# The first 20 microseconds of a streaming encoder: norm of the memory tokens, weight splits and bias tables in another order

## The chip, the cores and the metric

The kernel runs on one core of a Trainium2 chip. A time is that of the device for one launch, in microseconds. The core has five engines with a queue of instructions each, worked off in order: TensorE (PE: matmuls and transposes into PSUM), VectorE (DVE), ScalarE (ACT), GpSimd (POOL) and SyncE (SP), which issues most of the DMA transfers; POOL issues some too. An engine waits at an instruction until its operands are there, and everything behind it in that queue waits with it.

## The reference

One layer of a hybrid encoder on 2048 prompt frames and 8 x 16 sample frames, D_MODEL = 1024, all in float32. The part that matters here comes first in the kernel and is small:

```
def memory_kv(mem, g_mem, w_mk, w_mv):      # mem: 256 tokens x 1024
    m = rmsnorm(mem, g_mem)                 # mem * rsqrt(mean(mem^2) + EPS) * g_mem
    mk = (m @ w_mk).reshape(B, N_MEM, MEM_HEADS, MEM_HEAD_DIM)
    mv = (m @ w_mv).reshape(B, N_MEM, MEM_HEADS, MEM_HEAD_DIM)
    return mk, mv
```

After it come the projections of the frames, chunked band attention with a bias looked up by relative distance (`rel_bias`, 8 heads x 257), a causal depthwise convolution, the output projection, cross-attention into mk and mv, and a SwiGLU feed-forward layer.

## The kernel before

Float32 products are made of three matmuls: each operand is split into a high part (rounded to the type that TensorE takes at full rate) and a low part (the rest), and `mm3` (lines L281 to L283) adds high x high, high x low and low x high in PSUM. So each weight block of 128 x 1024 is loaded into one of three buffers `wf`, ScalarE makes the high part (`wload`, L275), and VectorE or GpSimd the low part (L276).

The phases follow each other: memory tokens (`phase_mem`), projections (`phase_proj`), attention, output projection, cross-attention, feed-forward. The instructions of all phases are given to a planner that simulates a timeline, with its own costs, and writes each engine's order; so the source's order is not the chip's, and work of a later phase may stand between that of an earlier one. `issue_after(x)`, which the changed kernel uses, forces an order: what is written under it comes behind instruction x on x's engine.

`phase_mem` does this:

- SP loads token tile 0 (128 tokens x 1024), the norm weight `g_mem_kv` spread over 128 partitions by a broadcasting transfer of 512 KB (`gain`, L360), token tile 1, and then blocks of `w_mk`.
- For each tile, `prenorm` squares and sums the rows on ScalarE (L306), makes the rsqrt on GpSimd (L298, L299), scales by it and by the norm weight on VectorE (L313), transposes eight 128 x 128 pieces on TensorE into one PSUM tile of 4 KB per partition (L316), and splits all eight at once: high part by ScalarE (L317), low part by VectorE (L318).
- For each of the eight blocks of `w_mk`, 24 matmuls (8 x `mm3`) give 128 rows of the transposed keys for all 256 tokens. The sum goes to SBUF on VectorE (L406), is split again (L407, L408), and is transposed back for the output (L394, L396). The low parts of blocks 0 and 1 are made on GpSimd, those of the others on VectorE.
- The keys are multiplied with `w_mqT`, head by head: 8 pieces of 6 matmuls per head, whose sums VectorE copies out (L426), and each head's 1 MB is stored to DRAM as `f1s` (L427). The output buffer exists twice, so head 2 waits for the store of head 0. Then the same for `w_mv` and `w_mo`.

`bias_tables` makes the table for the relative bias: SP loads the reversed bias (L249), VectorE builds rows of 767 values (L250 to L252), SP stores them to DRAM as `fd` (L254), and GpSimd issues a copy DRAM to DRAM (L259) that spreads them to `toep`, 2.5 MB, which attention reads much later. `phase_proj` halves the convolution's weights and two norm vectors on VectorE (L459, L461). The planner put both among the first instructions of VectorE.

Of the kernel before, what the change touches and what calls it, by code (L numbers as in the profile page):

```python
# [8 lines left out]
F32 = mybir.dt.float32  # L9
# [3 lines left out]
ALU = mybir.AluOpType  # L13
# [4 lines left out]
P = 128  # L18
D = 1024
# [6 lines left out]
NM = 256  # L26
# [14 lines left out]
MID = 4  # L41
TR0 = [12, 8]
MM = [12, 14, 4, 6]
HP = 100
HP2 = 200

# [90 lines left out]
class Build:  # L137
# [107 lines left out]
    def bias_tables(self, pool):  # L245
        nc, A = self.nc, self.A
        fb = self.t(pool, [H, 768], F32, "fb")
        rv = self.t(pool, [H, 256], F32, "rv")
        nc.sync.dma_start(rv[:, :], A["rel_rev"])  # L249
        nc.vector.memset(fb[:, :511], 0.0)  # L250
        nc.vector.tensor_scalar(fb[:, :511], fb[:, :511], rv[:, 0:1], None, ALU.add)
        nc.vector.tensor_copy(fb[:, 511:767], rv[:, :])  # L252
        fd = self.t(self.dpool, [H, 768], F32, "fd")
        nc.sync.dma_start(fd[:, :767], fb[:, :767])  # L254

        yield
        toep = self.t(self.dpool, [H, P, 5 * P], F32, "toep")
        f0 = fd[0, :]
        nc.gpsimd.dma_start(toep[:, :, :], bass.AP(f0.tensor, f0.offset + 127, [[768, H], [-1, P], [1, 5 * P]]))  # L259
        self.toep = [toep[h] for h in range(H)]  # L260
# [4 lines left out]
            return A[name + "_sample"][:, :]  # L265
        return A[name + "_prompt"][t * P:(t + 1) * P, :]

    def wload(self, src, hi=None, lo=None):
        nc = self.nc
        wf = self.t(self.w, [P, D], F32, "wf")  # L270
        self.last_load = nc.sync.dma_start(wf[:, :], src)
        if hi is None:
            hi = self.t(self.w, [P, D], F32R, "wh")
            lo = self.t(self.w, [P, D], F32R, "wl")
        nc.scalar.copy(hi[:, :], wf[:, :])  # L275
        self.lo_engine.tensor_tensor(lo[:, :], wf[:, :], hi[:, :].bitcast(F32), ALU.subtract)  # L276
        return hi, lo

    def mm3(self, ps, lh, ll, rh, rl, start, stop, **kw):
# [40 lines left out]
    def prenorm_halves(self, pool, pspool, xt, gbc, hi, lo):  # L320

        nc = self.nc
        r = self.rms(pool, xt[:, :])
        nc.vector.scalar_tensor_tensor(xt[:, :], xt[:, :], r[:, :], gbc[:, :], ALU.mult, ALU.mult)
        for k0 in range(0, KC, 4):
            ps = self.t(pspool, [P, 4, P], F32, "tr")
            for k in range(4):
                nc.tensor.transpose(ps[:, k, :], xt[:, (k0 + k) * P:(k0 + k + 1) * P], self.ident[:, :])
            sl = slice(k0, k0 + 4)
            nc.scalar.copy(hi[:, sl, :], ps[:, :, :])  # L330
            nc.vector.tensor_tensor(lo[:, sl, :], ps[:, :, :], hi[:, sl, :].bitcast(F32), ALU.subtract)

    def postnorm(self, pool, y, xt, gbc, dst, dma=None, bufs=2):
        nc = self.nc
# [28 lines left out]
    def phase_mem(self):  # L363
        nc, A = self.nc, self.A
        fa, fb = self.fa, self.fb
        pool = (Region().lay(self.sbF, 26, ("xt", 4, 2), ("gbc", 4, 1), ("yf", 1, 3), ("fb", 3, 1), ("rv", 1, 1))
                .lay(self.sbF, 24, ("junk", 2, 1)).lay(fb, 0, ("f1o", 8, 2))
                .lay(fa, 0, ("f2o", 8, 2), ("ot", 4, 2), ("ss", 0.03125, 6), ("rstd", 0.03125, 6))
                .lay(self.sbR, 24, ("mh", 8, 1), ("ml", 8, 1), ("yh", 8, 2), ("yl", 8, 2)))
        ps_mm = ps_tr = self.psa  # L370
        self.lo_engine = nc.vector
        xts = []
        for i in range(2):
            xt = self.t(pool, [P, D], F32, "xt", 2)
            nc.sync.dma_start(xt[:, :], A["mem_prompt"][i * P:(i + 1) * P, :])
            xts.append(xt)
            if i == 0:
                gbc = self.gain(pool, "g_mem_kv", "gbc")
        tables = self.bias_tables(pool)
        mh = self.t(pool, [P, KC, NM], F32R, "mh")  # L380
        ml = self.t(pool, [P, KC, NM], F32R, "ml")
        for i in range(2):
            self.prenorm(pool, ps_tr, xts[i], gbc, mh[:, :, i * P:(i + 1) * P], ml[:, :, i * P:(i + 1) * P])
        for which, wn, on in ((0, "w_mk", "new_mem_k_prompt"), (1, "w_mv", "new_mem_v_prompt")):
            yh = self.t(pool, [P, KC, NM], F32R, "yh", 2)
            yl = self.t(pool, [P, KC, NM], F32R, "yl", 2)
# [9 lines left out]
                    nc.scalar.copy(ot[i][:, j * P:(j + 1) * P], pt[:, i, :])  # L396

            for j in range(KC):
                self.lo_engine = nc.gpsimd if which == 0 and j < 2 else nc.vector
                wh, wl = self.wload(A[wn][j])  # L400
                ps = self.t(ps_mm, [P, 512], F32, "mm")
                for k in range(KC):
                    c = slice(k * P, (k + 1) * P)
                    self.mm3(ps[:, :NM], wh[:, c], wl[:, c], mh[:, k, :], ml[:, k, :], k == 0, k == KC - 1)
                yf = self.t(pool, [P, NM], F32, "yf", 3)
                nc.vector.tensor_copy(yf[:, :], ps[:, :NM])  # L406
                nc.scalar.activation(yh[:, j, :], yf[:, :], AF.Copy, scale=scale)  # L407
                nc.vector.scalar_tensor_tensor(yl[:, j, :], yf[:, :], scale, yh[:, j, :].bitcast(F32),  # L408
                                               ALU.mult, ALU.subtract)
# [36 lines left out]
    def phase_proj(self):  # L446
# [14 lines left out]
        nc.vector.tensor_scalar(half[:, :, :], cvec[:, 1:3, :], 0.5, None, ALU.mult)  # L461
        us = self.t(pool, [P, 4, DEC_B, HALO + DEC_S], F32, "us")

        def conv_halo():
# [1233 lines left out]
```

## Time and profile before

| what | us |
|---|---|
| median of 3 runs | 3012.31 (3011.44 to 3014.95) |
| the profiled execution | 3017.42 |
| its span, first to last instruction | 3015.6 |
| TensorE busy in the span | 2946.0 (98%) |
| VectorE busy | 2137.0 (71%) |
| ScalarE busy | 1358.3 (45%) |
| GpSimd busy | 1418.9 (47%) |

The tables of the profile name a group of instructions by line, engine, operation, output<-input and shape; `sbf`, `sbr`, `sbx` and `flexb` are the arenas in SBUF, `psb` is PSUM. Where a row of groups has two numbers and a bar, they are busy time and mean duration in ns, and behind the bar stands the idle time of the engine before them with what ended it. A timeline row has start and duration in us. A row of stretches has each engine's busy time and count, then the granted clock of TensorE (1.00 is full; before the first record of the clock, 1.00 is shown too), the mean busy share of the 16 DMA engines and the rate in GB/s.

### The profile page before, as it was taken

Reading aid. Unit: us, or ns where it says so; the run is one execution under the profiler, and the core shown is the slowest. Engines: PE = TensorE matmul, PEld = TensorE weight load, DVE = VectorE, ACT = ScalarE, POOL = GpSimd, SP = SyncE. Lnnn points to the kernel's source line nnn. Section 1 sums busy time; section 2 is a strip of 40 time slices with the busy share of each in tenths; the row PEclk is TensorE's granted clock in tenths of the full one; section 3 lists DMA queues with packets and bytes.
Section 4 is the critical chain, followed back from the end, with each engine's and each line's share of the span. In section 5 each row is a group of like instructions: output and inputs, shape, how many; then the busy total and the mean of one; then the engine's idle time right before and its main releaser. Section 6 shows DMA issues by size and latency. Waiting matters only on the chain.

```text
span 3015.6 us, 46098 instructions
## 1 busy us (share of the span) xinstructions
PE 2946.0 (98%) x16924; PEld 2712.9 (90%) x16924; DVE 2137.0 (71%) x3086; ACT 1358.3 (45%) x2729; POOL 1418.9 (47%) x1338
## 2 busy tenths in 40 slices
PE   7999999979999999999999999999999999999998
PEld 7999999969998888788878999999999999888887
DVE  6697795857786466535357887888788999655566
ACT  4535365657785345323334333433334444433433
POOL 1267496721113234226356655555555775524413
PEclk9999999989899999999999999999999999999999
DMA  8635353644534556324246433444434445756674
GB/s 295 246 112 179 96 165 110 202 167 172 181 135 153 175 190 216 128 68 147 74 166 210 138 128 132 166 166 153 154 125 160 144 139 187 260 187 207 220 230 149
DMA packets 197695, 500.10 MB, mean 166 GB/s; under 512 B 19349, under 2 KB 84765, under 8 KB 188627
## 3 DMA queue, kind: packets, MB, share of 16 engines
q1 hardware_dynamic: 182539, 427.53, 42.9%
q0 software_dynamic: 14928, 69.61, 6.2%
q8 instruction: 133, 2.18, 0.3%
q14 instruction: 95, 0.78, 0.1%
HBM read 365.97 MB, written 141.81 MB: 168 GB/s over the span
## 4 chain that ended last, share of the span: by engine, by line
PE 38%; DMA 4%; DVE 3%; issue 3%; POOL 3%; ACT 0%; SPq 0%; DVEq 0%; POOLq 0%; ACTq 0%
PE psb L283 12%; PE psb L282 12%; PE psb L281 12%; DMA sbf<-in_w_down_dram 2%; POOL sbf L1538 1%; PE psb L289 1%; DMA sbf<-x 1%; PE psb L1393 1%; DVE sbr L1416 0%; DMA sbf<-in_w_gate_dram 0%; DVE sbr L1608 0%; POOL sbf L338 0%; DMA hn<-sbf 0%; DVE sbr L1542 0%; DVE flexb L1478 0%
## 5 line engine op out<-in xcount | busy, mean ns | idle before, releaser
L281 PE MATMUL psb<-sbr 128*128 128x384 f32 (+3 forms) x2808 | 942.6, 337 | 4.1 <-DVE flexb L426 1.4
L282 PE MATMUL psb<-sbr 128*128 128x384 f32 (+3 forms) x2356 | 806.2, 342 | 3.4 <-DVE sbr L318 3.3
L283 PE MATMUL psb<-sbr 128*128 128x512 f32 (+3 forms) x1848 | 632.8, 344 | 3.7 <-DVE sbr L1608 3.6
L281 PEld LDWEIGHTS psb<-sbr 128*128 128x128 f32 x2808 | 530.9, 189 | 33.9 <-DVE flexb L426 2.1
L283 PE MATMUL psb<-sbr,sbx 128*128 128x384 f32 (+2 forms) x1484 | 477.2, 322 | 0.0
L282 PEld LDWEIGHTS psb<-sbr 128*128 128x128 f32 x2356 | 445.5, 189 | 30.6 <-DVE sbr L318 3.6
L283 PEld LDWEIGHTS psb<-sbr 128*128 128x128 f32 x1848 | 348.0, 189 | 33.2 <-DVE sbr L1608 6.3
L289 PE MATMUL psb<-sbr 128*128 128x512 f32 x1200 | 295.3, 394 | 2.7 <-POOL sbr L1251 1.4
L1416 DVE TENSOR_TENSOR sbr<-sbf,sbr 128x512 fp32r<-128x512 f32 x258 | 262.5, 1020 | 38.6 <-ACT sbr L1415 37.7
L1415 ACT CAST sbr<-sbf 128x512 fp32r<-128x512 f32 x258 | 159.3, 620 | 278.7 <-PE psb L282 228.8
L283 PEld LDWEIGHTS psb<-sbr,sbx 128*128 128x128 f32 x1484 | 281.2, 190 | 0.1
L523 DVE SCALAR_TENSOR_TENSOR psb<-sbf,psb 128x768 f32<-128x768 f32 (+1 forms) x290 | 264.3, 911 | 6.2
L289 PEld LDWEIGHTS psb<-sbr 128*128 128x128 f32 x1200 | 222.2, 189 | 48.5 <-POOL sbr L1251 1.8
L1608 DVE TENSOR_TENSOR sbr<-sbf,sbr 128x384 fp32r<-128x384 f32 (+2 forms) x242 | 166.4, 711 | 93.6 <-ACT sbr L1607 92.4
L276 POOL TENSOR_TENSOR sbx<-sbf,sbr 128x1024 fp32r<-128x1024 f32 x62 | 158.7, 2563 | 79.9 <-ACT sbr L275 76.4
L1607 ACT CAST sbr<-sbf 128x384 fp32r<-128x384 f32 (+2 forms) x242 | 112.4, 483 | 171.6 <-PE psb L282 149.4
L1538 POOL TENSOR_TENSOR sbf<-sbf 128x512 f32<-128x512 f32 x77 | 107.0, 1392 | 165.5 <-DMA sbf<-in_w_down_dram 163.6
L533 POOL TENSOR_TENSOR flexb<-flexb,flexb 128x128 f32<-128x128 f32 (+1 forms) x180 | 169.4, 942 | 23.1 <-ACT flexb L532 12.3
L281 PE MATMUL psb<-sbr,sbx 128*128 128x384 f32 (+1 forms) x524 | 170.6, 327 | 1.5 <-ACT sbx L1415 0.8
L1415 ACT CAST sbx<-sbf 128x512 fp32r<-128x512 f32 x153 | 94.7, 620 | 162.2 <-PE psb L282 147.4
L1416 DVE TENSOR_TENSOR sbx<-sbf,sbx 128x512 fp32r<-128x512 f32 x153 | 155.3, 1016 | 16.3 <-ACT sbx L1415 16.0
L1410 POOL TENSOR_TENSOR sbf<-sbf 128x512 f32<-128x512 f32 x66 | 96.9, 1468 | 107.3 <-DVE sbr L1416 50.5
(339 smaller groups left out, 6269.2 us busy)
## 6 DMA issues: line engine op xcount, KB each, us to landing
af<-flexb SPq DMA_DIRECT2D x33, 1344.0 KB, 5.7
sbf<-in_w_down_dram SPq DMA_DIRECT2D x154, 256.0 KB, 3.8
sbf<-in_w_gate_dram SPq DMA_DIRECT2D x66, 512.0 KB, 3.5
sbf<-in_w_up_dram SPq DMA_DIRECT2D x66, 512.0 KB, 3.9
sbf<-af SPq DMA_DIRECT2D x85, 384.0 KB, 4.1
sbf<-x SPq DMA_DIRECT2D x49, 512.0 KB, 4.0
sbf<-in_w_in_dram SPq DMA_DIRECT2D x48, 512.0 KB, 4.1
sbr<-ks POOLq DMA_DIRECT2D x16, 1024.0 KB, 8.5
```

Of the source, the lines that this page charges most:

```text
L276: self.lo_engine.tensor_tensor(lo[:, :], wf[:, :], hi[:, :].bitcast(F32), ALU.subtract)
L281: nc.tensor.matmul(ps, lh, rh, start=start, stop=False, **kw)
L282: nc.tensor.matmul(ps, lh, rl, start=False, stop=False, **kw)
L283: nc.tensor.matmul(ps, ll, rh, start=False, stop=stop, **kw)
L289: nc.tensor.matmul(y[o], l, r[:, o * 512:(o + 1) * 512], start=start and x == 0, stop=stop and x == 2)
L523: nc.vector.scalar_tensor_tensor(acc if w < CW - 1 else o, src(w), cwt[:, j, w:w + 1], acc, ALU.mult, ALU.add)
L533: nc.gpsimd.tensor_tensor(o, o, v, ALU.add)
L1415: nc.scalar.copy(hs[j][:, :], src[j])
L1416: nc.vector.tensor_tensor(ls[j][:, :], src[j], hs[j][:, :].bitcast(F32), ALU.subtract)
L1538: nc.gpsimd.tensor_tensor(acc[:, :], acc[:, :], q[:, :], ALU.add if s > 0 else ALU.subtract)
L1607: nc.scalar.copy(ch[:, m], a[:, x, m])
L1608: nc.vector.tensor_tensor(cl[:, m], a[:, x, m], ch[:, m].bitcast(F32), ALU.subtract)
```

## The change

- The norm weight is loaded as one row of 4 KB, first in SP's queue, and the two token tiles come right behind it. Two matmuls of a column of ones (1 x 128) with the row (1 x 512 each) spread it over 128 partitions in PSUM, where VectorE reads it when it scales.
- TensorE makes six transposes of the identity, with no use of the result, before these two matmuls and six after them.
- The tokens are transposed and split by PSUM bank: four pieces, then a high part and a low part of 128 x 512 (`prenorm_halves`, which `phase_proj` already uses), instead of eight and 128 x 1024.
- The low part of `w_mk` block 0 is made in two halves on GpSimd; those of block 1 (from GpSimd) and block 2 go to VectorE. High and low parts of blocks 1 and 2 are put behind the last splits of the tokens on ScalarE and VectorE.
- The load for the bias table comes after the loads for the first `w_mqT` head, and the three VectorE instructions of the table come after the last sum of the `w_mk` product; so the store of `fd` and the copy to `toep` come later too. In the order written for SP the load moves from place 7 to 22 and the store from 17 to 30.
- The halving of the convolution's vectors is put behind the last sum of the `w_mv` product.

Apart from these, the planner's order differs around the place where attention meets the output projection (some 200 matmuls, and instructions of ScalarE, VectorE and SP beside them), with the same instructions in it.

```diff
+WARM = (6, 0, 6)
...
-        nc.sync.dma_start(rv[:, :], A["rel_rev"])
-        nc.vector.memset(fb[:, :511], 0.0)
-        nc.vector.tensor_scalar(fb[:, :511], fb[:, :511], rv[:, 0:1], None, ALU.add)
-        nc.vector.tensor_copy(fb[:, 511:767], rv[:, :])
+        with self.tc.issue_after(self.last_load.ins):
+            nc.sync.dma_start(rv[:, :], A["rel_rev"])
+        with self.tc.issue_after(self.first_sum.ins):
+            nc.vector.memset(fb[:, :511], 0.0)
+            nc.vector.tensor_scalar(fb[:, :511], fb[:, :511], rv[:, 0:1], None, ALU.add)
+            nc.vector.tensor_copy(fb[:, 511:767], rv[:, :])
...
-    def wload(self, src, hi=None, lo=None):
+    def wload(self, src, hi=None, lo=None, parts=1):
...
-        self.lo_engine.tensor_tensor(lo[:, :], wf[:, :], hi[:, :].bitcast(F32), ALU.subtract)
+        for c in (slice(0, 512), slice(512, D)) if parts == 2 else (slice(0, D),):
+            self.lo_engine.tensor_tensor(lo[:, c], wf[:, c], hi[:, c].bitcast(F32), ALU.subtract)
...
     def phase_mem(self):
...
+        gain = self.t(pool, [1, D], F32, "gain")
+        nc.sync.dma_start(gain[:, :], A["g_mem_kv"].unsqueeze(0))
         xts = []
         for i in range(2):
             xt = self.t(pool, [P, D], F32, "xt", 2)
             nc.sync.dma_start(xt[:, :], A["mem_prompt"][i * P:(i + 1) * P, :])
             xts.append(xt)
-            if i == 0:
-                gbc = self.gain(pool, "g_mem_kv", "gbc")
+        ones = self.t(pool, [1, P], F32, "ones")
+        nc.vector.memset(ones[:, :], 1.0)
+        gbc = self.t(Region().lay(self.ps, 0, ("gbc", 4, 1)), [P, D], F32, "gbc")
+        warm = self.t(Region().lay(self.ps, 4, ("warm", 0.5, 1)), [P, P], F32, "warm")
+        event = None
+        for o in range(3):
+            with self.tc.issue_after(event.ins) if event else ExitStack():
+                for _ in range(WARM[o]):
+                    nc.tensor.transpose(warm[:, :], self.ident[:, :], self.ident[:, :])
+            if o < 2:
+                oc = slice(o * 512, (o + 1) * 512)
+                event = nc.tensor.matmul(gbc[:, oc], ones[:, :], gain[:, oc], start=True, stop=True)
...
-            self.prenorm(pool, ps_tr, xts[i], gbc, mh[:, :, i * P:(i + 1) * P], ml[:, :, i * P:(i + 1) * P])
+            splits = self.prenorm_halves(pool, ps_tr, xts[i], gbc, mh[:, :, i * P:(i + 1) * P], ml[:, :, i * P:(i + 1) * P])
...
-                self.lo_engine = nc.gpsimd if which == 0 and j < 2 else nc.vector
-                wh, wl = self.wload(A[wn][j])
+                self.lo_engine = nc.gpsimd if which == 0 and j == 0 else nc.vector
+                with ExitStack() as behind:
+                    for event in splits if which == 0 and j in (1, 2) else ():
+                        behind.enter_context(self.tc.issue_after(event.ins))
+                    wh, wl = self.wload(A[wn][j], parts=2 if which == 0 and j == 0 else 1)
...
-                nc.vector.tensor_copy(yf[:, :], ps[:, :NM])
+                self.first_sum = nc.vector.tensor_copy(yf[:, :], ps[:, :NM])
...
-        nc.vector.tensor_scalar(cwt[:, :, :], cwt[:, :, :], 0.5, None, ALU.mult)
         half = self.t(pool, [P, 2, 4], F32, "half", 1)
-        nc.vector.tensor_scalar(half[:, :, :], cvec[:, 1:3, :], 0.5, None, ALU.mult)
+        with self.tc.issue_after(self.first_sum.ins):
+            nc.vector.tensor_scalar(cwt[:, :, :], cwt[:, :, :], 0.5, None, ALU.mult)
+            nc.vector.tensor_scalar(half[:, :, :], cvec[:, 1:3, :], 0.5, None, ALU.mult)
```

More of the change, by code (lines that the diff above doesn't have):

```diff
@@ L329, in prenorm_halves @@
             sl = slice(k0, k0 + 4)
-            nc.scalar.copy(hi[:, sl, :], ps[:, :, :])
-            nc.vector.tensor_tensor(lo[:, sl, :], ps[:, :, :], hi[:, sl, :].bitcast(F32), ALU.subtract)
+            last = (nc.scalar.copy(hi[:, sl, :], ps[:, :, :]),
+                    nc.vector.tensor_tensor(lo[:, sl, :], ps[:, :, :], hi[:, sl, :].bitcast(F32), ALU.subtract))
+        return last
     def postnorm(self, pool, y, xt, gbc, dst, dma=None, bufs=2):
@@ L365, in phase_mem @@
         fa, fb = self.fa, self.fb
-        pool = (Region().lay(self.sbF, 26, ("xt", 4, 2), ("gbc", 4, 1), ("yf", 1, 3), ("fb", 3, 1), ("rv", 1, 1))
-                .lay(self.sbF, 24, ("junk", 2, 1)).lay(fb, 0, ("f1o", 8, 2))
+        pool = (Region().lay(self.sbF, 26, ("xt", 4, 2), ("gain", 4, 1), ("yf", 1, 3), ("fb", 3, 1), ("rv", 1, 1))
+                .lay(self.sbF, 23, ("ones", 0.5, 1)).lay(self.sbF, 24, ("junk", 2, 1)).lay(fb, 0, ("f1o", 8, 2))
                 .lay(fa, 0, ("f2o", 8, 2), ("ot", 4, 2), ("ss", 0.03125, 6), ("rstd", 0.03125, 6))
```

## The prediction

> **What bounds the kernel now.** I read the page first, then TensorE's waits in the first 140 us, then the timeline of those microseconds.
>
> ```profile
> span 3015.6 us, 46098 instructions
> PE 2946.0 (98%) x16924; PEld 2712.9 (90%) x16924; DVE 2137.0 (71%) x3086; ACT 1358.3 (45%) x2729; POOL 1418.9 (47%) x1338
> ```
>
> TensorE is busy for 98% of the span, so work off TensorE is hidden unless TensorE waits for it; what starts TensorE's stream earlier is worth its full length at the end, if no later wait swallows it. The waits of TensorE, from start to 140 us (in total, times, longest):
>
> ```profile
> PE psb L316 <- DVE sbf L313: 9.3, 2, 8.0
> PE psb L282 <- DVE sbr L318: 3.3, 1, 3.3
> PE psb L281 <- DVE flexb L426: 1.4, 2, 0.9
> PE psb L281 <- ACT sbr L317: 1.1, 1, 1.1
> ```
>
> 13.7 us lie before the first long run of matmuls (9.3 + 3.3 + 1.1), all in the norm of the memory tokens; 1.4 us come later, in the products with w_mqT. The timeline (start, duration, engine; in brackets the idle time and what ended it):
>
> ```profile
> 0.72 0.39 SPq L375 DMA_DIRECT2D sbf<-in_mem_prompt_dram  x1
> 1.17 0.42 SPq L360 DMA_DIRECT2D sbf<-in_g_mem_kv_dram  x1
> ...
> 4.60 1.06 ACT L306 ACTIVATE sbf<-sbf 128x1024 bf16<-128x1024 f32 x1 [2.60 <-DMA sbf<-in_mem_prompt_dram]
> 6.70 1.28 DVE L313 SCALAR_TENSOR_TENSOR sbf<-sbf,flexb 128x1024 f32<-128x1024 f32 x1 [5.22 <-POOL flexb L299]
> 7.79 1.06 ACT L306 ACTIVATE sbf<-sbf 128x1024 bf16<-128x1024 f32 x1 [2.04 <-DMA sbf<-in_mem_prompt_dram]
> 8.04 1.97 PE L316 MATMUL psb<-ident,sbf 128*128 128x128 f32 x8 [8.04 <-DVE sbf L313]
> 9.01 1.04 ACT L275 CAST sbr<-sbf 128x1024 fp32r<-128x1024 f32 x1
> 9.89 1.28 DVE L313 SCALAR_TENSOR_TENSOR sbf<-sbf,flexb 128x1024 f32<-128x1024 f32 x1 [1.91 <-POOL flexb L299]
> 12.23 1.51 DVE L251 TENSOR_SCALAR sbf<-sbf 8x511 f32<-8x511 f32 x1
> 13.67 0.27 DVE L252 COPY sbf<-sbf 8x256 f32<-8x256 f32 x1
> ...
> 15.13 2.37 DVE L461 TENSOR_SCALAR sbf<-sbf 128x8 f32<-128x8 f32 x1
> 17.36 1.21 DVE L318 TENSOR_TENSOR sbr<-psb,sbr 128x1024 fp32r<-128x1024 f32 x1
> 18.62 0.58 PE L282 MATMUL psb<-sbr 128*128 128x256 f32 x1 [3.31 <-DVE sbr L318]
> 19.00 0.41 PE L283 MATMUL psb<-sbr,sbx 128*128 128x256 f32 x1
> ...
> 22.84 0.41 PE L283 MATMUL psb<-sbr,sbx 128*128 128x256 f32 x1
> ...
> 23.33 0.28 PE L283 MATMUL psb<-sbr,sbx 128*128 128x256 f32 x1
> ...
> 26.08 0.28 PE L283 MATMUL psb<-sbr,sbx 128*128 128x256 f32 x1
> ```
>
> Between the two squares stand 3.2 us, since the broadcast norm weight (512 KB) sits between the two token tiles in SP's queue. The second tile's transposes were done at 13.2, but VectorE, which is in order, gave its low part only from 17.36: the bias table (L251, L252), a weight's split and the convolution's vectors (L461) stood ahead. The stream starts at 18.62 (three matmuls had gone before), and it runs at half speed for its first 4.4 us: 18 steps from 19.00 to 22.84 are 0.213 us each, 23 steps from 23.33 to 26.08 0.119.
>
> **The change, part by part.** *The stream's start.* In full-speed terms it now starts at 20.2: 18.62, less 0.4 for the three matmuls done, plus 4.4 us x 0.44 = 2.0 for the slow clock. Afterwards:
>
> ```profile
> L330 ACT CAST sbr<-psb x34: 573/587/603, 105.8 to 472.4; 128x512 fp32r<-128x512 f32 x34
> ...
> L331 DVE TENSOR_TENSOR sbr<-psb,sbr x34: 677/684/693, 106.5 to 473.2; 128x512 fp32r<-128x512 f32 x34
> ...
> L276 POOL TENSOR_TENSOR sbx<-sbf,sbr 128x1024 fp32r<-128x1024 f32 x62 | 158.7, 2563 | 79.9 <-ACT sbr L275 76.4 <-PE psb L328 2.9
> ...
> 5.00:10.00 5.00, 1.96 (x8) 1.57 (x8) 1.39 (x2) 2.89 (x5) 1.74 (x6) 1.00 1.00 390
> ```
>
> The 4 KB weight row goes first in SP's queue, so tile 0 is issued 0.45 us later: square at 5.05, VectorE 7.15, first transposes 8.49 (each row above plus 0.45). The two spreading matmuls: nothing in the trace has their shape (128x512 f32, one row deep). At the slow clock they lie between 0.43 us each (as a 256-column matmul of the stream doubled) and 0.85 (a 128-column f32 transpose takes 1.97/8 = 0.21 or so, so 512 columns four times that); at 0.85 and a row landing like a 512 KB tile they would end at 6.3, no later than the scale needs them. They cost nothing; cover is the square and the rsqrt (5.05 to 7.1). Without that cover 1.7 us. Tile 1 follows tile 0 at once: at the 390 GB/s of the last row (a stretch of 5 us; the last number is the DMA rate) 512 KB are 1.3 us, square at 6.35, second scale right behind the first on VectorE at 8.5 (before 9.89). The weight cast ends at 8.65.
>
> Then bank by bank: bank 0 of tile 0 is out at 9.5 (4 x 0.21 + 0.17), ScalarE 9.55 to 10.1, VectorE low part to 10.8; bank 1 low part to 11.7. Each of the two PSUM buffers must be free of its low part before tile 1 may be transposed into it, so tile 1's banks are out at 11.9 and 12.8, high parts at 12.55 and 13.4, low parts at 13.3 and 14.1. The first weight's split on POOL, now two halves of 1.3 to 2.0 each from 8.7 (ends 10.5 and 12.3), is ready. The first matmul goes at 12.6, the steady stream at 13.3. The splits of the next weights, put behind the last low part, (1.21 each on VectorE, as L318 of the same size, after 14.1) are ready at 15.6 and 16.8, before the 24 matmuls of a column (2.9 us each) ask for them. How long the clock stays slow then is not in this trace. Before, it took 4.4 us from the end of a 3.3 us gap; now the last gap of over 0.5 us ends at 10.9, so the same 4.4 us end at 15.3, 2.0 us into the stream, and cost 2.0 x 0.44 = 0.9. So 13.3 - 0.1 + 0.9 = 14.1: a gain of **6.1 us** (ends 5.0, with the 4.4 us counted from the stream, and 7.9, with no slow clock and so faster banks).
>
> *The idle transposes* (12 x 0.21 = 2.6 us on an idle TensorE, 6 before the row lands and 6 after) cost nothing, since TensorE has nothing else till 8.49. What they bring is the clock. After them TensorE idles again from about 6 to 8.5, so I give them nothing in the sum. Does such work raise the clock at all? The stretches around 640 us:
>
> ```profile
> 623.88:627.29 3.41, 2.56 (x11) 2.16 (x12) 0.77 (x2) 2.15 (x7) 0.00 (x0) 0.50 0.01 2
> ...
> 627.29:630.70 3.41, 1.64 (x7) 0.84 (x5) 2.66 (x5) 1.90 (x5) 1.13 (x2) 0.50 0.15 56
> ...
> 658.01:661.42 3.41, 3.41 (x16) 3.41 (x16) 1.63 (x4) 2.28 (x7) 0.52 (x1) 0.50 1.05 383
> 661.43:664.84 3.41, 2.60 (x18) 2.03 (x17) 2.18 (x7) 3.41 (x10) 0.10 (x1) 1.00 0.91 323
> ...
> 658.01:661.42 3.41, 2.54 (x11) 1.95 (x10) 0.00 (x0) 0.00 (x0) 0.50 1.05 383
> ```
>
> (The last column but two is the granted clock; the last row holds the transposes alone.) 2.56 us of transposes in the first stretch of 3.41 did not lift the clock from 0.5 in the second; a full stretch (the third), 2.54 us of it transposes, was followed by 1.0. So transposes count, but a stretch has to be nearly full. [...]
>
> *Tables moved behind.* Three VectorE instructions (0.48 + 1.51 + 0.27 = 2.26 us with the memset) leave the start and stand behind the last w_mk sum, among the copies of the w_mqT products; rel_rev's load and the fd store go 15 places back on SP, the toep copy follows on POOL, and nothing that TensorE needs in the next 20 us stands behind it there.
>
> ```profile
> L250 DVE MEMSET sbf<- 8x511 f32 x1 | 0.5, 484 | 0.9 <-PEq L1687 0.9
> ...
> L426 DVE COPY flexb<-psb x32: 410/416/425, 46.3 to 70.7; 128x256 f32<-128x256 f32 x32
> ...
> 59.35 0.42 DVE L426 COPY flexb<-psb 128x256 f32<-128x256 f32 x1 [1.84 <-DMA f1s<-flexb]
> ```
>
> Per head VectorE has 8 copies of 0.42 and two splits of 1.21, 5.8 us, beside 48 matmuls of 0.119 = 5.7: no room. Of the 2.26 us four PSUM buffers can take up at most three tiles, 2.1 us, if VectorE does not lag already, and nothing if it lags by that much; I take the middle, a stall of 1.3. But the 1.4 us stall of before, for the f1s store at 59.35, comes one head later and the store's place in the queue behind the new_mem_k output does not move, so it goes. Net **-0.1** (ends -1.4 and +2.3).
>
> *The toep copy* moves its traffic:
>
> ```profile
> q0 software_dynamic: 1040, 2.63, 33.2%
> ...
> 65.00:80.00 15.00, 15.00 (x128) 15.00 (x127) 11.25 (x19) 8.20 (x14) 1.19 (x3) 1.00 0.97 341
> 80.00:85.00 5.00, 5.00 (x44) 5.00 (x44) 4.61 (x6) 4.15 (x9) 1.20 (x2) 1.00 0.07 18
> ...
> 73.87 1.23 DVE L276 TENSOR_TENSOR sbx<-sbf,sbr 128x1024 fp32r<-128x1024 f32 x1 [1.34 <-ACT sbr L275]
> ```
>
> From 20 to 41 us it took 33.2% of 16 engines, 7.0 us of all DMA time. On the old clock it would now start near 59 (behind the fd store, itself behind the output), where the DMA share (last number but one) is already 0.97; only at 80 is there air. The split at 73.87 is that of the fourth w_mv block. Up to its cast, 1.05 us earlier, the copy takes 13.8 x 0.33 = 4.6 us from its load; the split ends at 75.1, and TensorE needs it after the last of the 32 copies, at 70.7 + 3 x 2.86 = 79.3: slack 4.2. I take the difference, **+0.4** (ends 0 and 7.0, all its DMA time).
>
> *The rest.* Halving the convolution's vectors goes behind the last w_mv sum: off the path, as convolution starts after 140 us; before it the 2.37 us of L461 was mostly a wait for loads. Some instructions where attention meets the output projection (900 to 990 us) change places; TensorE waits there only
>
> ```profile
> PE psb L877 <- DVE sbf L883: 1.4, 1, 1.4
> ```
>
> so I take 0 (ends -1.4, +1.4). Sum: -6.1 - 0.1 + 0.4 = **-5.8 us**. The profiled execution took 3017.42 us (span 3015.6), 5.1 over the median of the runs, 3012.31; the same 5.8 off the median gives **3006.5**.
>
> **The rivals.** *The clock is up early*: the idle transposes and spreading matmuls fill a stretch, and the clock lasts or returns before 12.4. Then the start gains 7.9 and the whole -7.6: 3004.7. For it: TensorE would be nearly always busy from 1.4 to 6. Against: the idle 2.5 us after; 2.56 busy of 3.41 did not do above.
> *The toep copy takes TensorE's loads*: all 7.0 us of DMA time fall on loads that TensorE waits for, and the 1.3 us VectorE stall stays: -6.1 + 1.3 + 7.0 = +2.2, slower, 3014.5. It decides once the copy costs TensorE more than 4.8 us. For it: the DMA share of 0.97. Against: the slack, and 0.07 at 80.
> *The queueing behind does nothing for the stream*: tile 1 or the fourth w_mk block comes late whatever VectorE does, because its load waits on SP for the first block's buffer, which POOL frees at 12.3 (before 13.4), and the stream stalls again at about 17; half of the gain is left, -2.9: 3009.4. For it: 1.1 us earlier on SP against 5.3 earlier in the stream. Against: three w_mk blocks, 8.6 us of matmuls, are there first.
>
> **How the numbers follow.** Within 0.2%, 6.0 us, counts as no change, about what a measurement can tell here. My forecast 0.55 (own range 3004.5 to 3009), the clock 0.20, the late tile 0.12, the toep copy 0.13. The forecast's range lies across the 0.2% line at 3006.3: about half of it is faster, 0.28, with the clock's 0.20 makes 0.48; a third of the toep case goes beyond 3018.3 if the reordered stretch at 900 us adds its waits: slower 0.06; same 0.46. Range 3003.0 (the clock, and the 1.4 us stall gone too) to 3012.5.
>
> **What would show it.** First L281 near 12.6 and a steady stream from 13.3; matmuls at 0.28 us from about 15.3; one stall of about 1 us in the w_mqT copies, none for f1s; toep from about 53 us on, w_mv casts waiting for DMA without TensorE waiting. The prediction is wrong if TensorE waits for w_mv splits between 65 and 85, if the stream breaks before 25, or if waits at 900 to 990 exceed 3 us.

## The result and the profile after

The changed kernel takes 3020.04 us (median of 11 runs, 3016.69 to 3025.05) against 3012.31 (11 runs) for the kernel before: a ratio of **1.0023**, 95% interval 1.0013 to 1.0034. It is slower, by 4 to 10 us. The forecast was 3006.5 us, with a range of 3003.0 to 3012.5 and a chance of 0.06 for a slower kernel: the time went the other way. The profiled execution took 3018.70 us. The page, and TensorE's waits in the first 140 us:

```profile
span 3016.9 us, 46136 instructions
PE 2949.0 (98%) x16940; PEld 2713.0 (90%) x16940; DVE 2134.6 (71%) x3090; ACT 1359.9 (45%) x2731; POOL 1415.6 (47%) x1338
```

```profile
PE psb L285 <- DVE flexb L446: 10.4, 2, 10.2
PE psb L392 <- POOL ident masks.py:199: 1.4, 1, 1.4
PE psb L332 <- DVE sbr L335: 0.7, 2, 0.6
...
PE psb L285 <- ACT sbr L334: 0.2, 1, 0.2
```

The 13.7 us of waits at the start are gone, as forecast (2.6 are left; part of the rest is filled by the idle transposes and the spreading matmuls, so the gain is read from when the stream starts). In their place stands one wait of 10.2 us for VectorE's copies of the w_mqT sums (L446, L426 before), of which 1.4 us had been there. The timeline of the start:

```profile
1.35 1.54 PE L392 MATMUL psb<-ident 128*128 128x128 f32 x6 [1.35 <-POOL ident masks.py:199]
2.82 3.78 PE L395 MATMUL psb<-sbf 1*128 1x512 f32 x4
4.57 1.06 ACT L310 ACTIVATE sbf<-sbf 128x1024 bf16<-128x1024 f32 x1 [2.57 <-DMA sbf<-in_mem_prompt_dram]
5.87 1.06 ACT L310 ACTIVATE sbf<-sbf 128x1024 bf16<-128x1024 f32 x1
6.53 1.54 PE L392 MATMUL psb<-ident 128*128 128x128 f32 x6
6.83 2.47 DVE L328 SCALAR_TENSOR_TENSOR sbf<-sbf,flexb,psb 128x1024 f32<-128x1024 f32 x2 [5.34 <-POOL flexb L303]
8.16 1.95 PE L332 MATMUL psb<-ident,sbf 128*128 128x128 f32 x8
12.02 0.38 PE L285 MATMUL psb<-sbr 128*128 128x256 f32 x1
12.74 0.39 PE L286 MATMUL psb<-sbr 128*128 128x256 f32 x1 [0.34 <-DVE sbr L335]
12.96 0.28 PE L287 MATMUL psb<-sbr,sbx 128*128 128x256 f32 x1
```

The steady stream starts at 12.74 (18.62 before), and from its second matmul on they last 0.28 us: no slow phase. So the start went better than forecast. Where the gain went, by the rows of 46 to 71 us:

```profile
46.55 1.32 POOL L262 DMA_DIRECT2D toep<-fd  x1 [34.52 <-DMA fd<-sbf]
...
49.75 0.55 SPq L447 DMA_DIRECT2D f1s<-flexb  x1
50.48 0.42 DVE L446 COPY flexb<-psb 128x256 f32<-128x256 f32 x1 [0.76 <-DMA f1s<-flexb]
...
55.95 0.53 SPq L447 DMA_DIRECT2D f1s<-flexb  x1
...
68.09 1.42 DVE L446 COPY flexb<-psb 128x256 f32<-128x256 f32 x4 [10.78 <-DMA f1s<-flexb]
```

VectorE stands for 10.78 us at its first copy of head 3, because the buffer's last content, head 1, is still on its way to f1s: issued at 49.75, landed at 68.00, 18.2 us. Just ahead of it, at 46.55, GpSimd had issued the toep copy, which landed at 67.78. These rows (by tile) give the flight of the f1s stores, shortest, median, longest. They count only the stores for which an engine waited: one in the kernel before (first row), and in the changed one (second row) those of heads 0 and 1, 6.5 us for the store issued ahead of the copy and 18.2 for the one behind it:

```profile
DMA to landing us min/median/max: 7.0/7.0/7.0
```

```profile
DMA to landing us min/median/max: 6.5/12.4/18.2
```

A w_mv load came late in the same stretch, but TensorE, back at 68.57 with VectorE's copies, did not wait for it:

```profile
69.36 1.05 ACT L278 CAST sbr<-sbf 128x1024 fp32r<-128x1024 f32 x1 [13.30 <-DMA sbf<-in_w_mv_dram]
```

For a table over all kernels I pair ScalarE's instructions from the last one backwards with those of the kernel before (their number differs only in the first microseconds) and take the median difference within 8 us around a time of the trace of before: the *stand*, negative when ahead. The changed kernel stands at -8.1 at 40 us, -8.3 at 60, +2.4 at 80, and +2.3 from 140 to 500. (TensorE's own instructions, paired the same way, stand at -7.6 from 25 to 55 us; read the values at 40 to within 1 us.) A second loss comes where attention meets the output projection, 900 to 1000. There the kernels ran at half clock for 0 to 6.8 us, and that changes from trace to trace of the same kernel (6.8 and 0 us in the two of the changed one; before 3.4), so the column in brackets takes half of the difference in half-clock time out.

| kernel | ratio to before, 95% interval | 40 us | 200 us | 900 to 1000, (at like clock) |
|---|---|---|---|---|
| changed | 1.0023 (1.0013 to 1.0034) | -8.1 | +2.3 | +4.2 (+2.5) |
| changed, again | 1.0032 (1.0021 to 1.0044) | -8.1 | +2.0 | +0.9 (+2.6) |
| tables early (e1) | 0.9984 (0.9974 to 0.9994) | -6.0 | -4.2 | -1.3 (+0.4) |
| before, tables behind (e2) | 1.0024 (1.0015 to 1.0034) | -3.6 | +8.1 | +2.5 (+2.5) |
| no idle transposes (e3) | 1.0011 (1.0003 to 1.0020) | -7.4 | +4.8 | +2.6 (+2.6) |
| wide store (e4) | 1.0013 (1.0003 to 1.0024) | -7.1 | +3.6 | +2.5 (+2.5) |
| toep late (e5) | 0.9989 (0.9976 to 1.0003) | -6.2 | -6.9 | +1.0 (+2.7) |
| tables early, toep late (e6) | **0.9973** (0.9963 to 0.9983) | -7.3 | -9.1 | +1.8 (+0.1) |
| before, toep late (e7) | 1.0007 (0.9996 to 1.0017) | -1.4 | -3.6 | +4.3 (+2.6) |

### The profile page after: what moved, and what is told of

It reads as the page before. It is cut to its first block, busy times and chain, and to the rows that moved or that the text cites. A ratio compares the mean times of both kernels' runs of the same rounds, so it can differ in the third digit from the quotient of the medians.

```text
span 3016.9 us, 46136 instructions
## 1 busy us (share of the span) xinstructions
PE 2949.0 (98%) x16940; PEld 2713.0 (90%) x16940; DVE 2134.6 (71%) x3090; ACT 1359.9 (45%) x2731; POOL 1415.6 (47%) x1338
## 5 line engine op out<-in xcount | busy, mean ns | idle before, releaser
L293 PEld LDWEIGHTS psb<-sbr 128*128 128x128 f32 x1200 | 222.6, 189 | 48.9 <-DVE flexb L1067 2.0
L280 POOL TENSOR_TENSOR sbx<-sbf,sbr 128x1024 fp32r<-128x1024 f32 (+1 forms) x62 | 154.6, 2496 | 82.1 <-ACT sbr L278 78.5
L1559 POOL TENSOR_TENSOR sbf<-sbf 128x512 f32<-128x512 f32 x77 | 106.9, 1393 | 166.6 <-DMA sbf<-in_w_down_dram 164.6
L278 ACT CAST sbr<-sbf 128x1024 fp32r<-128x1024 f32 x98 | 102.6, 1050 | 109.3 <-PE psb L286 51.4
```

The source lines that it names most:

```text
L280: self.lo_engine.tensor_tensor(lo[:, c], wf[:, c], hi[:, c].bitcast(F32), ALU.subtract)
L293: nc.tensor.matmul(y[o], l, r[:, o * 512:(o + 1) * 512], start=start and x == 0, stop=stop and x == 2)
L1559: nc.gpsimd.tensor_tensor(acc[:, :], acc[:, :], q[:, :], ALU.add if s > 0 else ALU.subtract)
```

## The experiments

T1 is my theory: the toep copy, moved into the flight of the f1s stores, makes one of them late, and VectorE and TensorE with it. T2: the planner's changed order where attention meets the output projection costs time. The changed kernel once more, as a measure beside e5 to e7:

> The changed kernel itself once more, as the measure for the three runs beside it, and for a second trace of it. All theories: slower than the kernel before by 0.1 to 0.35% (ratio 1.001 to 1.0035), TensorE's wait of about 10 us for VectorE's w_mqT copies, 3 to 5 us lost again at 900 to 1014 us against the kernel before.

It came out at 1.0032, as expected, with a wait of 10.3 us in the second trace. Between 900 and 1000 it loses 0.9 us, 2.6 at like clock, and not 3 to 5.

### e1: the bias table back at the front

```diff
-        with self.tc.issue_after(self.last_load.ins):
-            nc.sync.dma_start(rv[:, :], A["rel_rev"])
+        nc.sync.dma_start(rv[:, :], A["rel_rev"])
...
                 prev = (j, yf)
+                if which == 0 and j < 2:
+                    next(tables, None)
...
-                    next(tables, None)      # in the w_mqT loop
```

> The changed kernel, but rel_rev's load, the three VectorE steps of the bias table, the fd store and the toep copy go back to the front: they are issued from the w_mk loop (VectorE's steps behind the first w_mk sum, toep copy in flight from some 18 to 40 us). Every other part of the change stays. Theory T1 (the toep copy slows the f1s store, on which VectorE's copies and so TensorE wait): the wait of 10.4 us ahead of L285 at 61 to 71 us is gone, f1s of head 1 lands about 7 us after its issue as in the kernel before, the clock stays full there, and the gain of the start, some 8 us, lasts: about 3004 us, 8 below the kernel before (ratio 0.996 to 0.999). Theory T2 (the changed order of instructions where attention meets the output projection costs the time, and the start's gain is lost there): this kernel has the order of before in that place too, so it would also be fast; the next one but two, with the changed order, tells them apart. Rival R0 (the start's gain is worth nothing at the end, whatever happens at 60 us): 3012, as before, with the wait gone.

Ratio 0.9984: faster, but the stand at 200 is -4.2, not -8. The 10.2 us wait is gone (and head 1's store lands in 6.5 us); another has come, as TensorE's waits and ScalarE's timeline show (lines are lower by one here):

```profile
PE psb L284 <- DVE flexb L447: 3.5, 1, 3.5
```

```profile
42.09 1.04 ACT L277 CAST sbr<-sbf 128x1024 fp32r<-128x1024 f32 x1 [4.87 <-DMA sbf<-in_w_mqT_dram]
```

The copy now flies from 21.8 to 43.4, as in the kernel before, but the stream is 6 us earlier and asks for the w_mqT weights while the copy still holds their loads up: those whose landing is recorded land 5.4 to 7.7 us after their issue, and in e6, where the copy is gone from here, 4.2 to 4.4. TensorE also runs at half clock from 45.5 to 48.9 us, behind that wait. So T1's cause is right and its remedy was half right: at either place the copy meets something that the earlier stream needs.

### e2: the queueing of the tables alone, on the kernel before

The diff's two `issue_after` blocks around the bias table and the one around the convolution's vectors, nothing else.

> The kernel before with one part of the change alone: the bias-table steps and the halving of the convolution's vectors queued behind (rel_rev after the last weight load, VectorE's steps behind the sums, toep copy after them). T1: VectorE's low part of tile 1 comes 1.5 to 3 us earlier, so the start gains that, but the f1s store of some head meets the toep copy and the wait of VectorE for it grows from 1.4 to 8 to 12 us: 4 to 9 us slower than before, 3016 to 3021. Bandwidth shared without such a wait (the prediction's own view): 3009 to 3013.

Ratio 1.0024, 7.2 us of 3015, as T1 said. The start gains 3.6 us at 40 (VectorE's low part no longer stands behind the table), and then head 1's f1s store needs 18.4 us:

```profile
PE psb L283 <- DVE flexb L428: 10.6, 2, 10.2
...
PE psb L318 <- DVE sbf L315: 9.3, 2, 7.7
```

The first line is the wait of the changed kernel in a kernel that has nothing else of the change (its order where attention meets the output projection has come out changed too); the second is the old wait of the start. Moving the tables is enough to make the loss.

### e3: no idle transposes

```diff
-WARM = (6, 0, 6)
+WARM = (0, 0, 0)
```

> The changed kernel without the twelve idle transposes on the identity; the spreading matmuls stay. If the transposes raise the clock: it becomes full only some 3 to 5 us later, at about 14 to 16 us, the banks' transposes take twice as long, and the stream at 18 us stands 1.5 to 2.5 us behind the changed kernel; the wait for f1s at 60 to 70 us then shrinks by what the stream is late (the store's landing is set by the toep copy, not by TensorE), so the end moves by less than 1 us: 3019 to 3022. If the spreading matmuls alone raise it: full by 10 to 11 us all the same and no difference at all.

Ratio 1.0011. The clock is full from 14.4 us, as expected, but at 40 us the kernel is only 0.7 us behind the changed one, not 1.5 to 2.5. The wait did not shrink either (10.3 us), and half clock lasts to 75.9 us behind it, 3.4 us longer than in the changed kernel; at 200 it stands at +4.8. The interval overlaps that of the changed kernel; no loss shows in the time. More under e10.

### e4: the f1s store in runs of 8 KB

Same order of TensorE's and VectorE's instructions, the same bytes; only f1s lies as [P, MH, KC, NM], so a head's store writes one run per partition and not eight of 1 KB (cross-attention reads it in pieces of 1 KB).

```diff
-        self.f1s = self.dram("f1s", [P, KC, MH, NM])
+        self.f1s = self.dram("f1s", [P, MH, KC, NM])
```

> The changed kernel with f1s laid out so that each head's store writes one run of 8 KB per partition, not eight runs of 1 KB; everything else, the order of instructions on TensorE and VectorE included, stays. T1 with engines that take packets of the two queues in turn (R2): the store has fewer and larger packets, crosses the toep copy in 7 to 9 us, and VectorE's wait falls from 10.8 us to 2 or less: 3007 to 3012, 8 to 10 below the changed kernel. Shared bandwidth, or a conflict at the DRAM (R1, R3): the store lands 16 us or more after its issue as before, and nothing changes: 3018 to 3021. T2 (the order where attention meets the output projection): 3018 to 3021 whatever the store does, the time being lost at 900 to 1014 us.

The store does cross the copy now; the flights of heads 0 and 1, the second beside the copy:

```profile
DMA to landing us min/median/max: 5.1/7.2/9.3
```

and VectorE's wait is 1.4 us. The 1 MB store beside the copy landed in 9.3 us in runs of 8 KB, and in 18.2 in pieces of 1 KB: close to the 7 to 9 us that stood under R2, and far from the 16 or more under R1 and R3. So here it counted how the bytes are cut. That engines take packets in turn is not shown by it: the new layout changes the addresses too, so a conflict at the DRAM is not excluded. The packet counts in the last section agree with turns, without showing them. But the time moved by less than the noise (ratio 1.0013). The loss has gone elsewhere, which I had not expected. Waits, timeline and transfers of this kernel:

```profile
PE psb L411 <- DVE sbf L426: 5.5, 1, 5.5
```

```profile
73.70 1.04 ACT L278 CAST sbr<-sbf 128x1024 fp32r<-128x1024 f32 x1 [6.32 <-DMA sbf<-in_w_mv_dram]
```

```profile
sbf<-in_w_mv_dram SPq DMA_DIRECT2D x8, 512.0 KB, 8.1
toep<-fd POOLq DMA_DIRECT2D x1, 2560.0 KB, 31.6
```

Now the stream is not stopped at 58, the copy needs 31.6 us instead of 21.2, and ScalarE waits 6.3 us for a w_mv load, TensorE 5.5 behind it: the same work in the same stretch, another victim. In the changed kernel such a wait was hidden behind the store's.

### e5: the toep copy alone moved again, to where DMA has air

```diff
-        for _ in tables:
-            pass
+        self.tables = tables
...
+                if (gi, j) == (1, 1):           # second group of projections
+                    with self.tc.issue_after(halo.ins):
+                        next(self.tables, None)
```

The copy goes to where DMA has room, as the stretches of the changed kernel show (last number but one):

```profile
150.00:160.00 10.00, 10.00 (x63) 9.97 (x62) 8.06 (x8) 5.74 (x10) 6.20 (x7) 1.00 0.49 178
...
170.00:180.00 10.00, 10.00 (x59) 10.00 (x59) 9.79 (x11) 2.49 (x3) 3.05 (x2) 1.00 0.13 43
```

(`halo` is the GpSimd instruction that fills the convolution's edge; the w_mqT loop keeps the first step of `tables` only.)

> The changed kernel with the toep copy alone moved once more, behind a GpSimd instruction of the second group of projections (near 165 us, where the DMA share is 0.13 to 0.31); it is first read near 540 us. The order of instructions where attention meets the output projection is that of the changed kernel. T1 (the copy meets the loads and stores of the memory phase): no wait above 2 us ahead of L285, and at 200 us this kernel stands 8 to 9 us ahead of the one before; T2 (that order costs 3.8 us) comes on top: 4 to 6 us faster in the end, ratio 0.998 to 0.9987. T1 without T2: 8 to 9 us faster, 0.997. Rival R0 (DMA traffic of the memory phase is too much for the earlier stream, with or without the copy): weight loads come late, a stall of 3 us or more between 40 and 100 us stays, and the end is at -2 to +1 us.

The copy is issued at 155.5 and takes 19.0 us; nothing waits for it. All waits of TensorE in the first 140 us:

```profile
PE psb L285 <- ACT sbr L334: 1.6, 2, 1.4
PE psb L392 <- POOL ident masks.py:199: 1.4, 1, 1.4
PE psb L332 <- DVE sbr L335: 0.6, 1, 0.6
```

The f1s stores land in 6.2 to 6.4 us, and at 200 the stand is -6.9, 9.2 better than the changed kernel, but short of the 8 to 9 expected (here the clock is full only from 16.3 us, and a wait of 1.4 us for ScalarE stands in the first row). Ratio 0.9989; its interval reaches 1.0003, so alone it does not settle that this is faster than before, but it excludes the ratio of 1.0032 measured beside it. The DMA traffic of the memory phase is not too much for the earlier stream: R0 falls.

### e6: e5 with the table's small steps early

e1's edit on e5, for the first step of `tables` alone.

> The run before this one with rel_rev's load, the bias table's VectorE steps and the fd store back at the front of the w_mk loop, the toep copy near 165 us as there. What it is for: with these the instructions of TensorE from 100 us on stand exactly in the order of the kernel before, in the place where attention meets the output projection too. T1 and T2 both: 8 to 10 us faster than the kernel before (ratio 0.9967 to 0.9975), and 3 to 4 us faster than the run before this one, the difference lying at 900 to 1014 us. T2 false: as the run before this one, within 1.5 us.

Ratio 0.9973, some 8 us faster than the kernel before (median 3008.61 beside 3015.22) and the fastest of all that were timed more than once. Its page:

```profile
span 3006.6 us, 46142 instructions
PE 2948.7 (98%) x16940; PEld 2712.6 (90%) x16940; DVE 2131.7 (71%) x3090; ACT 1362.8 (45%) x2731; POOL 1417.2 (47%) x1338
```

Against e5 it gains 2.2 us before 200, and at 900 to 1000 it loses nothing at like clock, where e5 loses 2.7. TensorE does not wait there at all, while the changed kernel and e7 have these rows between 880 and 1020:

```profile
PE psb L293 <- DVE flexb L1067: 1.8, 2, 1.6
```

```profile
PE psb L289 <- DVE flexb L1049: 2.0, 2, 1.7
```

### e7: the kernel before with the toep copy late

> The kernel before with one edit: the toep copy goes behind the same GpSimd instruction near 165 us. Its start stays as it was; where attention meets the output projection its instructions come out in the order of the changed kernel. T2: slower than the kernel before by 2 to 4 us (ratio 1.0007 to 1.0013), lost at 900 to 1014 us. T2 false: within 1.5 us, or faster by up to 1.4 where the wait for f1s at 59 us goes.

1.0007, with an interval from 0.9996 to 1.0017: the time alone leaves it open. The trace does not: it stands at -3.6 at 200, so the copy cost the kernel before some 2 to 3 us as well (the 1.4 us wait for f1s is gone), and loses 2.6 at like clock between 900 and 1000. Its sum, -1.0, does not bear out the 2 to 4 us slower that T2 gave for this kernel, but the loss lies where T2 says. At like clock the seven traces above with the changed order there (in e2 and e5 a dozen matmuls differ from it) lose 2.5 to 2.7 us, the two with exactly the order of before 0.4 (e1) and 0.1 (e6). So T2's cause holds, at 2.5 us and not the 3.8 expected. About 1.6 to 2 us of it is the wait in the rows above; the rest is not traced to an instruction.

### e8 to e11: what the parts of the start are worth

One trace each, from e6, where no long wait downstream swallows the gain; read by the stand, not by the time.

> The fastest kernel so far (tables early, toep copy near 165 us; 9.1 us ahead of the kernel before at 200 us of its trace) with one part of the start undone: the norm weight is broadcast by a 512 KB load between the two token tiles again, and the two spreading matmuls are gone. What to read is the stand at 40 and at 200 us against the kernel before. If the spreading is what brings the second tile early, as the prediction has it: the second square is again some 3 us behind the first, and 2 to 4 of the 9 us are lost. If the low part's order on VectorE alone sets the start: under 1 us is lost.

> The same kernel with the transposes, high and low parts of a token tile whole again (8 transposes, then one copy and one subtraction over 1024 columns) in place of bank by bank. If the banks overlap TensorE, ScalarE and VectorE as the prediction has it: first main matmul 1 to 2 us later, and that is lost at 40 us. If the second tile waits for its first buffer anyway: under 0.5 us.

> The same kernel without the twelve idle transposes. The kernel it comes from had its clock full only from 14.4 us, as the changed kernel without idle transposes had: if they are worth nothing where the clock's windows fall so, the stand at 40 us is the same within 0.7 us; if they are worth something always, 1 to 2 us are lost.

> The same kernel without the queueing of the second and third weight's splits behind the token tiles' last parts. If the splits would go ahead of the low parts on VectorE (1.2 us each): the first main matmul or the steady stream is 1.2 to 2.4 us later, and lost at 40 us. If their weights come too late for that anyway: no difference above 0.3 us.

| undone in e6 | stand at 40 (lost) | at 200 (lost) | clock full from |
|---|---|---|---|
| nothing (e6) | -7.3 | -9.1 | 14.4 |
| norm weight by row and matmuls (e8) | -5.4 (1.9) | -7.5 (1.6) | 17.6 |
| bank by bank (e9) | -5.9 (1.4) | -8.1 (1.0) | 10.9 to 14.3, then 17.7 |
| idle transposes (e10) | -6.3 (1.0) | -8.8 (0.3) | 17.0 |
| later splits queued behind (e11) | -4.4 (2.9) | -4.2 (4.9) | 17.8 |

The queueing of two weight splits is worth the most of the four, 2.9 us at the start; I had given it no term of its own in the sum. The 4.9 lost at 200 are not all the start's: 2 us more go between 100 and 140, untraced. VectorE's timeline without the queueing shows why the start loses: the second weight's split (first and third row) goes ahead of the tokens' low parts, and the first main matmul comes at 15.40 and not at 12.47.

```profile
10.82 2.13 DVE L279 TENSOR_TENSOR sbx<-sbf,sbr 128x1024 fp32r<-128x1024 f32 x1 [1.52 <-ACT sbr L277]
12.88 1.27 DVE L334 TENSOR_TENSOR sbr<-psb,sbr 128x512 fp32r<-128x512 f32 x2
14.07 1.21 DVE L279 TENSOR_TENSOR sbx<-sbf,sbr 128x1024 fp32r<-128x1024 f32 x1
15.38 0.69 DVE L334 TENSOR_TENSOR sbr<-psb,sbr 128x512 fp32r<-128x512 f32 x1
```

e8 loses just under the 2 to 4 us expected; its squares are 3.4 us apart again (4.39 and 7.75). e9's clock was up from 10.9 us, but back at half from 14.3 to 17.7, in the stream, so its loss is not told apart from the clock's. e10 loses 1.0 at 40 and 0.3 at 200, between the two cases named for it. The clock alone makes some 1 us of difference, so terms of 1 us or less are not told apart here. Between 900 and 1000, e8 has the order of before and loses 0.0 at like clock; the others have the changed one (e9 but for a dozen matmuls) and lose 4.7 to 4.9, with a second wait of 1.7 us beside the one known.

## Why the prediction was wrong, point by point

**The stream's start (6.1 us, ends 5.0 and 7.9): right, a little small.** Measured 8.1 at 40 us (7.6 by TensorE's own instructions), some 1 us of it luck with the clock, as the next point shows. The tiles' squares came at 4.57 and 5.87 (forecast 5.05, 6.35), the first transposes at 8.16 (8.49), the first main matmul at 12.02 (12.6), the stream at 12.74 (13.3). One bound was wrong without harm: the two spreading matmuls take 3.78 us together and not up to 1.7; they end at 6.60, and the scale that reads them starts at 6.83.

**The idle transposes (nothing) and the rival "the clock is up early" (0.20).** In both traces of the changed kernel the rival came true: full clock from 9.96 and 9.88 us. But in four other kernels with the same twelve transposes and two matmuls (e1, e4, e5, e6) it was full from 14.4 to 16.3, and in e3, without the transposes, from 14.4. These four gain 6.0 to 7.3 us at 40 (5.8 to 6.6 by TensorE), as my sum had it; the early clock is worth about 1 us more, when it comes.

**The rival "the queueing behind does nothing for the stream" (0.12)**: false, by e11, which loses 2.9 us at 40 without it.

**Tables moved behind (-0.1).** The stall of 1.3 us did not come: TensorE's waits for VectorE there are 0.2 us beside the long one. VectorE's three instructions took 0.48, 0.22 and 0.47 us at 37.7 to 40.2; the 1.51 us of L251, on which I built, was not what it costs here. The other half of the term is the first step that failed: "the 1.4 us stall of before, for the f1s store ... so it goes". It grew to 10.2. I had seen that VectorE waits for this store, and took its flight of 7.0 us as given while moving a 2.5 MB copy next to it.

**The toep copy (+0.4, ends 0 and 7.0): the step that decides, and it failed twice.** First, in whom the copy delays: I weighed it against the w_mv loads and their slack of 4.2 us, and not against the f1s stores, which were in the air at the same time with no slack at all, since VectorE was already waiting for one. Second, in the bound: "all its DMA time" is no upper end. Here one queue's copy held up another queue's store by 11.2 us (18.2 less 7.0), where its own packets take 7.0 us of all engines:

```profile
55.00:60.00 5.00, 3.33 (x28) 3.13 (x27) 2.06 (x4) 1.05 (x1) 0.00 (x0) 1.00 1.04 394
60.00:65.00 5.00, 0.00 (x0) 0.00 (x0) 0.00 (x0) 0.00 (x0) 0.00 (x0) 0.62 0.60 238
65.00:70.00 5.00, 1.43 (x6) 1.43 (x7) 1.42 (x4) 0.64 (x1) 0.00 (x0) 0.50 0.71 257
```

From 60 to 65 none of these engines does anything, and yet DMA is busy for only 0.60 and moves 238 GB/s against 394 just before. A price in DMA time cannot see that. Then the clock: it was granted at half from 61.2 to 71.4, and the first 2.8 us of matmuls after the wait ran at that. From 60 to 80 us the kernel loses 10.6: 10.2 of wait, 1.4 of slow clock, less the 1.4 us wait of before, and 0.4 that I cannot place.

The rival "the toep copy takes TensorE's loads" (0.13, 3014.5) was the nearest: right cause and sign, decided where the copy costs more than 4.8 us, but with the wrong victim and too small a price. Its own victim does exist: with the stores made short, a w_mv load stops TensorE for 5.5 us (e4), and earlier in the kernel a w_mqT load for 3.5 (e1). The copy started at 46.55, earlier than the 53 to 59 I had.

**The rest (0, ends -1.4 and +1.4): wrong, +2.5 us.** I took the reordered stretch as free since the waits there were 1.4 us in all. The row that I showed for it (L877) lies at 881, ahead of the stretch; within it TensorE waited 0.2. A changed order is not bounded by the waits of the old one. The sign that I had named, over 3 us of waits, did not come either (1.8).

**Sum:** +2.3 at 200 and +2.5 for the order are +4.8; measured are 7 (4 to 10) and 10 (6 to 13) us, so 2 to 5 us are not placed. For the other timed kernels this sum (e1 -3.8, e2 +10.6, e3 +7.4, e4 +6.1, e5 -4.2, e6 -9.0, e7 -1.0) follows the measured ratios times 3015 (-4.8, +7.2, +3.3, +3.9, -3.3, -8.1, +2.1) to within 1 to 4 us. It leaves out 500 to 900 us. There the traces of all other kernels, both of the changed one too, gain 7 to 13 us on the one trace of the kernel before, which ran at half clock for 7 to 20 us longer in that stretch. That execution took 3017.42 us beside a median of 3012.31, so I take the difference for its own and not for a gain; with no second trace of the kernel before this is not shown.

Of what would show it right, the start came, and so did the w_mv casts that wait for DMA without TensorE waiting (the 13.30 us above); the missing f1s wait did not. Of what would show it wrong (TensorE waiting for w_mv splits at 65 to 85, a break before 25, waits at 900 to 990) nothing came: I had not put the store on that list.

## What to carry to other kernels

When a transfer is moved, list everything that is in flight in its new place, stores as much as loads, and who waits for each; a wait that is already there, however short, marks the transfer without slack. Price the meeting by packets and not by bytes alone: in this kernel the same 1 MB store landed 18.2 us after its issue beside the copy in pieces of 1 KB, and 9.3 us in runs of 8 KB. And a copy that is needed only much later belongs where DMA has room (0.13 to 0.49 busy near 165 us) rather than where the program happens to produce it: that one move is worth 9 us to the changed kernel at 200, and 2 to 3 to the one before.

## What the runs showed of the hardware

**Two queues in the same microseconds.** The DMA queues of the changed kernel from 61 to 66 us (q0 carries the toep copy, q1 the stores and loads of SP; packets, MB, share of 16 engines):

```profile
q0 software_dynamic: 169, 0.87, 41.4%
q1 hardware_dynamic: 182, 0.19, 10.4%
```

By these rows a packet of the copy takes 196 ns (0.414 x 16 x 5 us / 169), one of the store 46 ns, and both queues passed nearly the same number; taken singly, the four us from 62 on have 34, 34, 35 and 33 packets of the copy and 34, 35, 32 and 35 of SP's queue. Together 0.52 of 16 engines were busy, 8.3 of them. Two other stretches: from 58 to 60 us, where DMA is busy for 1.05, the copy passes 68 packets, as many in a us as later, and SP's queue 434; and from 22 to 24 us in the kernel before, with a single packet of SP's queue beside it, the copy's queue is busy for 53.1% of 16 engines. I read the five us as about eight engines that still had both, taking one packet of each in turn, and eight with nothing left. That is an estimate from these counts: which engine a packet ran on was not to be seen, and no run shows the turns. By it a 1 MB store in 1 KB packets, 64 for each of 16 engines, would need 64 x 0.242 = 15.5 us of the 18.2; in packets of 8 KB it would have 8, and e4's landed in 9.3.

**The clock after a start of transposes.** In the two traces of the changed kernel full clock came at 9.96 and 9.88 us. The 3.41 us before held 14 transposes, with TensorE busy for 3.32 of them; the 3.41 us before those were full too, of spreading matmuls, but full clock did not follow: the six transposes behind them took 1.54 us, as the six ahead of them had. (3.41 us is the length of the shortest stretch between two changes of the granted clock in the traces of the kernel before and the changed one: 0.50 from 685.80 to 689.21 us in the changed kernel, 1.00 on both sides.) e9 is a third such trace: 16 transposes, 3.32 us busy, from 7.5 to 10.9, and full clock from 10.9. So in these three traces full clock followed a stretch of transposes. In e5 it did not follow a stretch as busy (3.33 us, from 6.0 to 9.5), but 0.55 us of that was a spreading matmul; full clock came only at 16.3.

In nearly all traces of this case the 3.41 us just before the first full clock are busy for at least 3.04 us with transposes or main matmuls (3.41 in the kernel before, 3.32 in the changed one), and the earlier stretches, counted back in steps of 3.41 us, for at most 2.84. The exception is e10, where no full clock followed a stretch with 3.07 us. What sets the moment is not shown: no run changes the spreading matmuls, or where these stretches fall, by themselves.

**The type of the split parts.** In the first 23 us of the kernel before a 256-column matmul of split parts takes a step of 0.213 us, and eight 128-column transposes in float32 take 1.97 us, 0.25 each: more than twice as long for a column. TensorE ran no third type in this case, so this is all that shows what "full rate" is worth.
